# First channel block of a transformer layer modulated for two token tiles alone, with its value weights split in halves

## The chip, the cores and the metric

The kernel runs on one core of a Trainium2 chip. The metric is the device time of one execution in microseconds. One core has five engines that work side by side, each from a queue of its own: TensorE (matrix products and transposes; PE in the profile, with its weight loads as PEld), VectorE (DVE), ScalarE (ACT), GpSimd (POOL) and SyncE (SP), which here issues the loads and stores. TensorE writes to PSUM, and VectorE or ScalarE copy from there to SBUF.

## The reference, cut to what matters

One layer of a hybrid block over 512 latent tokens (`x`) and 256 context tokens (`ctx`) with 1024 channels. The part that the change touches is the start:

```python
mod = jax.nn.silu(c) @ ada_w[l] + ada_b[l]
sh1, sc1, g1, sh2, sc2, g2 = split(mod, 6)          # the same with c_ctx for the context tokens
hx = rmsnorm(x, norm1_g[l]) * (1 + sc1) + sh1        # (512, 1024)
hc = rmsnorm(ctx, norm1_g[l]) * (1 + csc1) + csh1    # (256, 1024)
v   = (hx @ w_in[l])[:, values]                      # (512, 512), one of the products with w_in
v_c = (hc @ w_in[l])[:, values]                      # (256, 512)
...
```

Then follow the other products with `w_in` (a Fourier mixer, a gated convolution, neighbourhood attention that reads the context keys too, three gates), the merged branches with an output product, a second modulated norm, a squared-ReLU MLP of width 4096 and a final norm.

## The kernel before

**Precision.** Every product is done in three matmuls (`mm3`, lines 82 to 84). Each operand is held as two parts, a high part (a cast, ScalarE, line 59 or 200) and a low part (the operand minus the high part, VectorE, line 60 or 201). Line 82 multiplies high by high, 83 high by low, 84 low by high.

**The head of the kernel.** Tokens are on partitions in tiles of 128: four latent tiles `xts` and two context tiles `cts`. `token_norm` takes a tile: ScalarE squares and sums it (148), VectorE and GpSimd make the reciprocal root (103, 104), VectorE scales the tile (150), TensorE turns it in two groups of four transposes (154), and VectorE copies the first group and ScalarE the second (155) to `xnT` (latent) or `cnT` (context), where channels are on partitions. Channels come in eight blocks of 128, numbered `m`.

Scale and shift of a block come in two steps. The row step `mod_rows(m)` is 16 matmuls with the weights `adaA[m]` (163) and a copy to SBUF `rsb` (166). The column step `mod_cols(m)` is four small matmuls that turn the rows (172) and two small VectorE instructions for `a1` and `b1` (173, 174). Then `modulate(m)` does block `m` for all tokens: one VectorE instruction (177), the cast (59) and the low part (60) to `hx` or `hc`. `values(m, wv, ts)` adds block `m` to the value products of the token tiles `ts`, three matmuls for each tile into one of six PSUM accumulators `vacc`.

The value weights come in loads of 1024 columns that serve two blocks: the first 512 columns block `m`, the others block `m + 1`; `halves` makes both parts of all 1024 (200, 201).

**Order before the loop.** Norms of latent tiles 0 and 1, row step of block 0, norms of tiles 2 and 3, column step of block 0, modulation of block 0 for all 512 tokens, parts of the first value weights. The loop over `m` then does in turn the loads for later blocks, the row step of block `m + 1`, the products of tiles 0 and 1, the column step and the modulation of block `m + 1`, and the products of tiles 2 and 3. At `m == 1` the context tiles are normed and join.

**What sets the order.** The program states dependences; a planner decides, when the kernel is built, in which order each engine gets its instructions. It goes by the order of the program among those that it reckons ready, so an instruction can stand in an engine's queue well ahead of its place in the text, as the cast of the value weights does (it is ahead of tile copies that are written before it). At run time each engine takes its queue strictly in that order. `tc.keep_in_program_order(ins)` ties an instruction to a place behind the one that was traced just before it on the same engine; it orders the queue and adds no wait for another engine.

**Loads.** SyncE issues them in its own order. The weights `adaA` go through four buffers, two for each block, so that the loads for block `m + 2` wait for the row step of block `m`; the value weights go through two buffers. The latent tiles and `adaA[0]` come first, then `wV[0]`, `adaA[1]`, `adaA[2]` and the context tiles.

Of the kernel before, what the change touches and what calls it, by code (L numbers as in the profile page):

```python
# [11 lines left out]
F32R = mybir.dt.float32r  # L12
AF = mybir.ActivationFunctionType
ALU = mybir.AluOpType
PSUM = bass.MemoryType.PSUM

P = 128
D = 1024
SEQ = 512
# [7 lines left out]
KD = D // P  # L27
# [3 lines left out]
HT = SEQ // 2  # L31
RAW = 4 * HALF
# [5 lines left out]
def dit_block(ctx: ExitStack, tc: tile.TileContext, a: dict):  # L38
    nc = tc.nc
    PE, V, S, G = nc.tensor, nc.vector, nc.scalar, nc.gpsimd  # L40

    def pool(stack, name, bufs, side=None, space=None):
        kw = {"reuse_waits": "tile"}
        if side:
            kw["side"] = side
        if space:
            kw["space"] = space
        return stack.enter_context(tc.tile_pool(name=name, bufs=bufs, **kw))
# [3 lines left out]
    wsp = pool(ctx, "wsp", 3)  # L52
    sgp = pool(ctx, "sgp", 3)

    def f(ap):
        return ap.bitcast(F32)

    def split(hi, lo, src):
        S.copy(hi, src)  # L59
        V.tensor_tensor(lo, src, f(hi), op=ALU.subtract)  # L60

    def weights(src, n=D):

        raw = wraw.tile([P, RAW], F32, tag="raw", name="raw")
        nc.sync.dma_start(raw[:, :n], src)
        w = weight_tile()
        split(w[:, 0, :n], w[:, 1, :n], raw[:, :n])
        return w
# [11 lines left out]
    def mm3(out, st, mv, start, stop, **kw):  # L80

        PE.matmul(out, st[0], mv[0], start=start, stop=False, **kw)  # L82
        PE.matmul(out, st[0], mv[1], start=False, stop=False, **kw)  # L83
        PE.matmul(out, st[1], mv[0], start=False, stop=stop, **kw)  # L84
# [17 lines left out]
    def rstd_of(ss, n):  # L102
        V.tensor_scalar(ss, ss, 1.0 / D, EPS, op0=ALU.mult, op1=ALU.add)  # L103
        G.tensor_tensor(ss, ss, mhalf[:, 0:n], op=ALU.pow)  # L104
# [7 lines left out]
    a1 = const.tile([P, KD, 2], F32, name="a1")  # L112
    b1 = const.tile([P, KD, 2], F32, name="b1")
# [3 lines left out]
    hx = hxp.tile([P, 2, KD, SEQ], F32R, name="hx")  # L117
# [19 lines left out]
    xnT = ph1.tile([P, KD, SEQ], F32, name="xnT")  # L137
    cnT = ph1.tile([P, KD, CTX], F32, name="cnT")

    def load(src, t):  # L140
        xt = ph1.tile([P, D], F32, tag="xt", name="xt", bufs=4)
        nc.sync.dma_start(xt, src[t * P:(t + 1) * P, :])
        return xt

    def token_norm(xt, t, dst):
        ss = ph1.tile([P, 1], F32, tag="ss", name="ss", bufs=3)
        junk = ph1.tile([P, D], mybir.dt.bfloat16, tag="junk", name="junk")
        S.activation(junk, xt, AF.Square, accum_out=ss)
        rstd_of(ss, 1)
        V.tensor_scalar(xt, xt, ss, None, op0=ALU.mult)  # L150
        for g in range(2):
            tp = ps1.tile([P, 4, P], F32, tag="acc", name="tp", bufs=6)
            for i in range(4):
                PE.transpose(tp[:, i, :], xt[:, (4 * g + i) * P:(4 * g + i + 1) * P], ident)
            (S.copy if g else V.tensor_copy)(dst[:, 4 * g:4 * g + 4, t * P:(t + 1) * P], tp)

    def mod_rows(m, w):


        rows = ps1.tile([P, 256], F32, tag="rows", name="rows")  # L160
        for k in range(KD):
            j = k % 4
            PE.matmul(rows[32 * j:32 * j + 32], sig32[:, k, :], w[k // 4][:, j * 256:(j + 1) * 256],
                      start=k < 4, stop=k >= 4)
        rsb = ph1.tile([P, 256], F32, tag="rsb", name="rsb", bufs=2)
        S.copy(rsb, rows)
        return rsb

    def mod_cols(m, rsb):
        cp = ps1.tile([P, 2, 2], F32, tag="cols", name="cp")  # L170
        for i in range(2):
            PE.matmul(cp[:, i, :], rsb[:, i * P:(i + 1) * P], comb, start=True, stop=True)
        V.tensor_scalar(a1[:, m, :], cp[:, 0, :], bsc1[:, m:m + 1], n1g[:, m:m + 1], op0=ALU.add, op1=ALU.mult)
        V.tensor_scalar(b1[:, m, :], cp[:, 1, :], bsh[:, m:m + 1], None, op0=ALU.add)

    def modulate(m, src, dst, j):
        V.tensor_scalar(src[:, m], src[:, m], a1[:, m, j:j + 1], b1[:, m, j:j + 1], op0=ALU.mult, op1=ALU.add)
        split(dst[:, 0, m], dst[:, 1, m], src[:, m])

    vacc = {}  # L180

    def values(m, w, ts):
        mv = [w[:, h, (m % 2) * 512:(m % 2 + 1) * 512] for h in range(2)]
        for t in ts:
            if m == 0:
                vacc[t] = ps1.tile([P, 512], F32, tag="acc", name=f"vacc{t}", bufs=6)
            if t < 4:
                st = [hx[:, h, m, t * P:(t + 1) * P] for h in range(2)]
            else:
                st = [hc[:, h, m, (t - 4) * P:(t - 3) * P] for h in range(2)]  # L190
            mm3(vacc[t], st, mv, m == 0, m == KD - 1)

    def fetch(src, p=rawx):
        raw = p.tile([P, RAW], F32, tag="raw", name="raw")
        nc.sync.dma_start(raw[:, :D], src)
        return raw[:, :D]

    def halves(raw):
        w = wsp.tile([P, 2, RAW], F32R, tag="w", name="w")
        S.copy(w[:, 0, :D], raw)  # L200
        V.tensor_tensor(w[:, 1, :D], raw, f(w[:, 0, :D]), op=ALU.subtract)
        return w

    def ada_fetch(m):
        return [fetch(a["adaA"][m, i]) for i in range(2)]

    xts = [load(a["x"], t) for t in range(2)]
    ada = ada_fetch(0)
    xts += [load(a["x"], t) for t in range(2, NT)]
    wn = fetch(a["wV"][0], wraw)  # L210
    w = ada
    ada = ada_fetch(1)
    token_norm(xts[0], 0, xnT)
    token_norm(xts[1], 1, xnT)
    rsb = mod_rows(0, w)
    token_norm(xts[2], 2, xnT)
    token_norm(xts[3], 3, xnT)
    mod_cols(0, rsb)
    modulate(0, xnT, hx, 0)
    wv = halves(wn)  # L220
    for m in range(KD):
        if m < KD - 1:
            w = ada
        if m % 2 == 1 and m < KD - 1:
            wn = fetch(a["wV"][(m + 1) // 2], wraw)
        if m < KD - 2:
            ada = ada_fetch(m + 2)
        if m == 0:
            cts = [load(a["ctx"], t) for t in range(NCT)]
        if m < KD - 1:  # L230
            rsb = mod_rows(m + 1, w)
        if m % 2 == 0 and m:
            wv = halves(wn)
        values(m, wv, range(2))
        if m < KD - 1:
            mod_cols(m + 1, rsb)
            modulate(m + 1, xnT, hx, 0)
        values(m, wv, range(2, 4))
        if m == 1:
            for t in range(NCT):  # L240
                token_norm(cts[t], t, cnT)
            modulate(0, cnT, hc, 1)
            modulate(1, cnT, hc, 1)
            values(0, wv, (4, 5))
        if m:
            values(m, wv, (4, 5))
            if m < KD - 1:
                modulate(m + 1, cnT, hc, 1)
    for t in range(6):
        src = vacc[t].rearrange("p (h d) -> p h d", d=HD)  # L250
        split(Vst[:, t, :, 0, :], Vst[:, t, :, 1, :], src)
# [63 lines left out]
    for g in range(2):  # L315
        w = weights(a["wU"][g])
# [19 lines left out]
    for c in range(2):  # L336
        pf = ps1.tile([P, 512], F32, tag="acc", bufs=6, name="pf")
        for half in range(2):
            for z in range(2):
                m = (0, 2 if half == 0 else 1)[z]  # L340
# [183 lines left out]
    for c in range(KD):  # L524
# [12 lines left out]
        w = weights(a["wM"][c])  # L537
# [67 lines left out]
    for kk in range(4):  # L605
        w = weights(a["wO"][0, kk])
# [9 lines left out]
    for kk in range(4):  # L616
        raw = wraw.tile([P, RAW], F32, tag="raw", name="raw")[:, :D]
        nc.sync.dma_start(raw, a["wO"][1, kk])
        w = wop.tile([P, 2, D], F32R, tag="wo", name="wo")
# [23 lines left out]
    def turned(t, xn):  # L643
        out = []
        for g in range(2):
            tp = psZ.tile([P, 4, P], F32, tag="d", name="tp2")
            for i in range(4):
                PE.transpose(tp[:, i, :], xn[:, (4 * g + i) * P:(4 * g + i + 1) * P], ident)
            out.append(tp)
        return out  # L650
# [282 lines left out]
    for ii in range(4):  # L933
        raw = wraw.tile([P, RAW], F32, tag="raw", name="raw")[:, :D]
        nc.sync.dma_start(raw, a["w2"][3, 1, ii])
        w = Sp.tile([P, 2, D], F32R, tag="S", name="wl", bufs=4)
        split(w[:, 0], w[:, 1], raw)
        ws.append(w)
    for t in range(NT):
        ss = sss[t]  # L940
# [110 lines left out]
```

## Time and profile before

| what | value |
|---|---|
| median of 3 runs | 802.93 us (802.64 to 803.0) |
| the profiled execution | 803.09 us, its span 801.3 us |
| TensorE matmuls, busy | 782.6 us (98%), 4484 instructions |
| VectorE, busy | 525.4 us (66%), 792 instructions |
| ScalarE, busy | 346.7 us (43%), 587 instructions |
| GpSimd, busy | 110.7 us (14%), 127 instructions |
| chain that ended last | TensorE 93%, VectorE 2%, ScalarE 2% |

Times in the views count from the start of the span. A row of the timeline has the start, the duration, the engine, the line of the kernel, the operation, the output and the inputs; in square brackets stands how long the engine was idle before and what ended that. Merged instructions carry their number (x8). A low share of an engine's busy time says nothing about a stretch in which another engine waits for it.

### The profile page before, as it was taken

How to read it: one execution, taken by the hardware profiler on the slowest of the kernel's cores; microseconds unless marked ns; L12 is line 12 of the kernel's file. 1: busy time of each engine (PE TensorE's matmuls, PEld its weight loads, DVE VectorE, ACT ScalarE, POOL GpSimd, SP SyncE). 2: the span in 40 equal slices, each digit the busy share in tenths (PEclk: the TensorE clock that was granted, in tenths of full speed). 3: DMA queues.
4: the chain of work that ended last, by engine and by line, in shares of the span. 5: the costliest groups of instructions: out<-in, count | busy, mean ns of one | idle time of the engine just before them, and what ended most of it. 6: DMA issues, size and time to landing. Idle time of an engine off the chain costs nothing.

```text
span 801.3 us, 11393 instructions
## 1 busy us (share of the span) xinstructions
PE 782.6 (98%) x4484; PEld 673.7 (84%) x4484; DVE 525.4 (66%) x792; ACT 346.7 (43%) x587; POOL 110.7 (14%) x127
## 2 busy tenths in 40 slices
PE   4999999999999999999999999999999999999996
PEld 3679988888888888888888999989888989998885
DVE  4655455997977898444358988656556666475973
ACT  5435334564782322323245475344543444334232
POOL 1000002221201000000000014222222222032000
PEclk9999999999999999999999999999999999999998
DMA  8654232332309897322443132223233333321312
GB/s 330 250 193 109 80 116 69 99 95 80 83 29 321 299 313 254 124 95 89 157 157 133 53 133 79 95 90 113 98 106 106 106 106 106 106 80 54 125 60 105
DMA packets 33654, 104.07 MB, mean 130 GB/s; under 512 B 8128, under 2 KB 8256, under 8 KB 33600
## 3 DMA queue, kind: packets, MB, share of 16 engines
q1 hardware_dynamic: 32832, 100.97, 36.9%
q0 software_dynamic: 768, 2.38, 1.5%
q8 instruction: 35, 0.57, 0.3%
q14 instruction: 19, 0.16, 0.1%
HBM read 98.87 MB, written 2.10 MB: 126 GB/s over the span
## 4 chain that ended last, share of the span: by engine, by line
PE 93%; DVE 2%; ACT 2%; issue 1%; DMA 1%; SPq 0%; POOL 0%; POOLq 0%; ACTq 0%
PE pd L82 7%; PE pd L83 7%; PE pd L84 7%; PE pg L84 6%; PE pg L83 6%; PE pg L82 5%; PE pA L84 3%; PE pA L82 3%; PE pA L83 3%; PE pu L83 2%; PE pu L82 2%; PE pu L84 2%; PE pbr L83 2%; PE pbr L84 2%; PE pbr L82 2%; PE vacc L82 2%
## 5 line engine op out<-in xcount | busy, mean ns | idle before, releaser
L60 DVE TENSOR_TENSOR w<-raw,w 128x1024 fp32r<-128x1024 f32 x87 | 108.1, 1243 | 54.3 <-ACT w L59 53.3
L59 ACT CAST w<-raw 128x1024 fp32r<-128x1024 f32 x87 | 91.2, 1048 | 83.0 <-PE pbr L84 27.4
L60 DVE TENSOR_TENSOR w<-rr,w 128x512 fp32r<-128x512 f32 (+1 forms) x65 | 66.6, 1044 | 72.0 <-ACT w L59 70.7
L83 PE MATMUL pd<-w,aT 128*128 128x512 f32 x224 | 87.8, 392 | 0.0
L84 PE MATMUL pd<-w,aT 128*128 128x512 f32 x224 | 87.6, 391 | 0.0
L82 PE MATMUL pd<-w,aT 128*128 128x512 f32 x224 | 85.8, 394 | 0.0
L59 ACT CAST w<-rr 128x512 fp32r<-128x512 f32 (+1 forms) x65 | 45.0, 707 | 78.1 <-POOL rr L780 34.7
L84 PE MATMUL pg<-hx,w 128*128 128x512 f32 x192 | 76.5, 398 | 0.0
L83 PE MATMUL pg<-hx,w 128*128 128x512 f32 x192 | 76.2, 397 | 0.0
L82 PE MATMUL pg<-hx,w 128*128 128x512 f32 x192 | 74.9, 390 | 0.0
L84 PEld LDWEIGHTS pd<-w,aT 128*128 128x128 f32 x224 | 42.0, 187 | 9.4
L83 PEld LDWEIGHTS pd<-w,aT 128*128 128x128 f32 x224 | 42.1, 188 | 9.0 <-DVE w L60 0.8
L82 PEld LDWEIGHTS pd<-w,aT 128*128 128x128 f32 x224 | 41.8, 188 | 8.2 <-ACT w L59 0.4
L82 PEld LDWEIGHTS pg<-hx,w 128*128 128x128 f32 x192 | 36.8, 192 | 8.0
L83 PEld LDWEIGHTS pg<-hx,w 128*128 128x128 f32 x192 | 36.1, 188 | 8.0
L517 DVE SCALAR_TENSOR_TENSOR acc<-ada,sig,acc 128x1024 f32<-128x1024 f32 x28 | 35.9, 1283 | 10.3 <-DMA ada<-in_adaB 10.0
L776 POOL TENSOR_TENSOR rr<-rr 128x512 f32<-128x512 f32 x13 | 17.3, 1333 | 183.4 <-DVE w L60 183.4
L84 PEld LDWEIGHTS pg<-hx,w 128*128 128x128 f32 x192 | 36.1, 188 | 7.2
L104 POOL TENSOR_TENSOR ss<-ss,mhalf 128x1 f32<-128x1 f32 x10 | 6.6, 660 | 224.5 <-DVE ss L103 224.5
L534 ACT ACTIVATE sg<-pg 128x512 f32<-128x512 f32 x21 | 12.5, 597 | 58.0 <-PE pg L84 57.9
L544 DVE TENSOR_TENSOR sg<-pbr,sg 128x512 f32<-128x512 f32 x24 | 16.5, 686 | 20.6 <-PE pbr L84 20.6
L84 PE MATMUL pA<-Sq,w 128*128 128x256 f32 x104 | 29.3, 282 | 0.0
(338 smaller groups left out, 2151.5 us busy)
## 6 DMA issues: line engine op xcount, KB each, us to landing
raw<-in_w SPq DMA_DIRECT2D x38, 512.0 KB, 3.5
ada<-in_adaB SPq DMA_DIRECT2D x32, 512.0 KB, 5.1
rr<-in_w SPq DMA_DIRECT2D x26, 512.0 KB, 4.0
raw<-in_wG SPq DMA_DIRECT2D x24, 512.0 KB, 3.4
raw<-in_adaA SPq DMA_DIRECT2D x16, 512.0 KB, 6.3
raw<-in_wM SPq DMA_DIRECT2D x8, 512.0 KB, 3.9
raw<-in_wO SPq DMA_DIRECT2D x8, 512.0 KB, 3.3
raw<-in_wC SPq DMA_DIRECT2D x6, 512.0 KB, 3.3
```

The source lines that it names most:

```text
L59: S.copy(hi, src)
L60: V.tensor_tensor(lo, src, f(hi), op=ALU.subtract)
L82: PE.matmul(out, st[0], mv[0], start=start, stop=False, **kw)
L83: PE.matmul(out, st[0], mv[1], start=False, stop=False, **kw)
L84: PE.matmul(out, st[1], mv[0], start=False, stop=stop, **kw)
L104: G.tensor_tensor(ss, ss, mhalf[:, 0:n], op=ALU.pow)
L517: V.scalar_tensor_tensor(acc[:, q, :], raw, sigv[:, k, 0:1], acc[:, q, :], op0=ALU.mult, op1=ALU.add)
L534: S.activation(sg, pg, AF.Sigmoid)
L544: V.tensor_tensor(pgs[b], pb, pgs[b], op=ALU.mult)
L776: G.tensor_tensor(ra[:, lo], ra[:, lo], rb[:, lo], op=ALU.add)
```

## The change

Latent tile 2 is normed and scaled, but not turned, before the row step of block 0. The parts of the first value weights are made in halves: the first 512 columns early, the others behind the modulation of the second 256 tokens. Block 0 is modulated in two halves of 256 tokens, the first (tiles 0 and 1) before tile 2 is turned. The products of tiles 0 and 1 with block 0 and the row step of block 1 leave the loop and stand between the turning of tiles 2 and 3. `token_norm` is taken apart into `squares`, `scaled` and `turned`; the square and the scaling of tile 3 and the copies of tiles 2 and 3 are pinned with `in_order`, each behind the instruction that is traced before it on its engine. The context tiles still go through `token_norm` as a whole, unpinned.

```diff
--- before.py
+++ after.py
@@ -59,6 +59,10 @@
         S.copy(hi, src)
         V.tensor_tensor(lo, src, f(hi), op=ALU.subtract)
 
+
+
+    in_order = tc.keep_in_program_order
+
     def weights(src, n=D):
 
         raw = wraw.tile([P, RAW], F32, tag="raw", name="raw")
@@ -142,17 +146,27 @@
         nc.sync.dma_start(xt, src[t * P:(t + 1) * P, :])
         return xt
 
-    def token_norm(xt, t, dst):
+    def squares(xt):
         ss = ph1.tile([P, 1], F32, tag="ss", name="ss", bufs=3)
         junk = ph1.tile([P, D], mybir.dt.bfloat16, tag="junk", name="junk")
-        S.activation(junk, xt, AF.Square, accum_out=ss)
+        return ss, S.activation(junk, xt, AF.Square, accum_out=ss)
+
+    def scaled(xt, ss):
         rstd_of(ss, 1)
-        V.tensor_scalar(xt, xt, ss, None, op0=ALU.mult)
+        return V.tensor_scalar(xt, xt, ss, None, op0=ALU.mult)
+
+    def token_norm(xt, t, dst):
+        scaled(xt, squares(xt)[0])
+        turned(xt, t, dst)
+
+    def turned(xt, t, dst):
         for g in range(2):
             tp = ps1.tile([P, 4, P], F32, tag="acc", name="tp", bufs=6)
             for i in range(4):
                 PE.transpose(tp[:, i, :], xt[:, (4 * g + i) * P:(4 * g + i + 1) * P], ident)
-            (S.copy if g else V.tensor_copy)(dst[:, 4 * g:4 * g + 4, t * P:(t + 1) * P], tp)
+            copied = (S.copy if g else V.tensor_copy)(dst[:, 4 * g:4 * g + 4, t * P:(t + 1) * P], tp)
+            if dst is xnT and t >= 2:
+                in_order(copied)
 
     def mod_rows(m, w):
 
@@ -173,9 +187,9 @@
         V.tensor_scalar(a1[:, m, :], cp[:, 0, :], bsc1[:, m:m + 1], n1g[:, m:m + 1], op0=ALU.add, op1=ALU.mult)
         V.tensor_scalar(b1[:, m, :], cp[:, 1, :], bsh[:, m:m + 1], None, op0=ALU.add)
 
-    def modulate(m, src, dst, j):
-        V.tensor_scalar(src[:, m], src[:, m], a1[:, m, j:j + 1], b1[:, m, j:j + 1], op0=ALU.mult, op1=ALU.add)
-        split(dst[:, 0, m], dst[:, 1, m], src[:, m])
+    def modulate(m, src, dst, j, t=slice(None)):
+        V.tensor_scalar(src[:, m, t], src[:, m, t], a1[:, m, j:j + 1], b1[:, m, j:j + 1], op0=ALU.mult, op1=ALU.add)
+        split(dst[:, 0, m, t], dst[:, 1, m, t], src[:, m, t])
 
     vacc = {}
 
@@ -212,14 +226,26 @@
     ada = ada_fetch(1)
     token_norm(xts[0], 0, xnT)
     token_norm(xts[1], 1, xnT)
+    scaled(xts[2], squares(xts[2])[0])
+
     rsb = mod_rows(0, w)
-    token_norm(xts[2], 2, xnT)
-    token_norm(xts[3], 3, xnT)
+    wv = wsp.tile([P, 2, RAW], F32R, tag="w", name="w")
+    S.copy(wv[:, 0, :512], wn[:, :512])
+    ss3, sq = squares(xts[3])
+    in_order(sq)
     mod_cols(0, rsb)
-    modulate(0, xnT, hx, 0)
-    wv = halves(wn)
+    V.tensor_scalar(xnT[:, 0, :HT], xnT[:, 0, :HT], a1[:, 0, 0:1], b1[:, 0, 0:1], op0=ALU.mult, op1=ALU.add)
+    V.tensor_tensor(wv[:, 1, :512], wn[:, :512], f(wv[:, 0, :512]), op=ALU.subtract)
+    split(hx[:, 0, 0, :HT], hx[:, 1, 0, :HT], xnT[:, 0, :HT])
+    turned(xts[2], 2, xnT)
+    in_order(scaled(xts[3], ss3))
+    rsb = mod_rows(1, ada)
+    values(0, wv, range(2))
+    turned(xts[3], 3, xnT)
+    modulate(0, xnT, hx, 0, slice(HT, SEQ))
+    split(wv[:, 0, 512:D], wv[:, 1, 512:D], wn[:, 512:])
     for m in range(KD):
-        if m < KD - 1:
+        if m:
             w = ada
         if m % 2 == 1 and m < KD - 1:
             wn = fetch(a["wV"][(m + 1) // 2], wraw)
@@ -227,11 +253,12 @@
             ada = ada_fetch(m + 2)
         if m == 0:
             cts = [load(a["ctx"], t) for t in range(NCT)]
-        if m < KD - 1:
+        elif m < KD - 1:
             rsb = mod_rows(m + 1, w)
         if m % 2 == 0 and m:
             wv = halves(wn)
-        values(m, wv, range(2))
+        if m:
+            values(m, wv, range(2))
         if m < KD - 1:
             mod_cols(m + 1, rsb)
             modulate(m + 1, xnT, hx, 0)
```

## Rows read from the trace of the kernel before

**Rows 1.** The page's busy times: us, share of the span, number of instructions.

```profile
PE 782.6 (98%) x4484; PEld 673.7 (84%) x4484; DVE 525.4 (66%) x792; ACT 346.7 (43%) x587; POOL 110.7 (14%) x127
```

**Rows 2.** Stretches: us; busy (instructions) PE, PEld, DVE, ACT, POOL; granted clock; DMA share; GB/s.

```profile
12.60:19.50 6.90, 5.20 (x55) 3.55 (x54) 5.82 (x13) 5.10 (x10) 1.10 (x2) 1.00 1.00 382
...
27.00:29.00 2.00, 1.70 (x12) 0.96 (x9) 1.68 (x3) 1.61 (x3) 0.28 (x1) 1.00 0.88 336
29.00:785.00 756.00, 755.17 (x4296) 652.28 (x4295) 505.19 (x747) 327.00 (x550) 104.41 (x109) 1.00 0.37 122
```

**Rows 3.** Timeline, TensorE's steps from 14 to 23 us.

```profile
14.08 1.09 PE L154 MATMUL tp<-ident,xt 128*128 128x128 f32 x8 [0.39 <-DVE xt L150]
...
15.01 0.51 PE L172 MATMUL cp<-cols,rsb 128*128 128x2 f32 x4
...
16.75 1.07 PE L163 MATMUL rows<-raw,sig 128*32 128x256 f32 x16
...
19.54 0.50 PE L82 MATMUL vacc<-w,hx 128*128 128x512 f32 x1 [0.61 <-ACT hx L59]
...
22.51 1.07 PE L163 MATMUL rows<-raw,sig 128*32 128x256 f32 x16
```

**Rows 4.** The same timeline, instructions around them from 12 to 21 us.

```profile
12.62 1.06 PE L163 MATMUL rows<-raw,sig 128*32 128x256 f32 x14
...
12.79 1.06 ACT L148 ACTIVATE junk<-xt 128x1024 bf16<-128x1024 f32 x1
...
14.31 0.38 ACT L166 COPY rsb<-rows 128x256 f32<-128x256 f32 x1
14.58 1.06 ACT L200 CAST w<-raw 128x1024 fp32r<-128x1024 f32 x1
14.86 0.75 DVE L150 TENSOR_SCALAR xt<-xt,ss 128x1024 f32<-128x1024 f32 x1 [0.73 <-POOL ss L104]
...
16.13 0.27 DVE L173 TENSOR_SCALAR a<-cp,bsc,cols 128x2 f32<-128x2 f32 x1
16.42 0.69 DVE L155 COPY xnT<-tp 128x512 f32<-128x512 f32 x1
...
17.03 0.21 DVE L174 TENSOR_SCALAR b<-cp,cols 128x2 f32<-128x2 f32 x1
17.16 1.21 DVE L201 TENSOR_TENSOR w<-raw,w 128x1024 fp32r<-128x1024 f32 x1
...
18.86 0.62 ACT L59 CAST hx<-xnT 128x512 fp32r<-128x512 f32 x1 [0.60 <-DVE xnT L177]
...
20.70 0.62 ACT L59 CAST hx<-xnT 128x512 fp32r<-128x512 f32 x1 [1.22 <-DVE xnT L177]
```

**Rows 5.** Groups by line and shape, first 50 us: count, busy us, mean ns.

```profile
L60 DVE TENSOR_TENSOR hx<-xnT,hx 128x512 fp32r<-128x512 f32 x6 | 4.1, 688 | 0.8 <-ACT hx L59 0.7
...
L59 ACT CAST hx<-xnT 128x512 fp32r<-128x512 f32 x6 | 3.7, 620 | 8.1 <-DVE xnT L177 8.1
...
L177 DVE TENSOR_SCALAR xnT<-xnT,a,b 128x512 f32<-128x512 f32 x6 | 3.3, 545 | 0.1
...
L177 DVE TENSOR_SCALAR cnT<-cnT,a,b 128x256 f32<-128x256 f32 x6 | 2.3, 408 | 0.0
...
L59 ACT CAST hc<-cnT 128x256 fp32r<-128x256 f32 x6 | 2.2, 406 | 0.0
L60 DVE TENSOR_TENSOR hc<-cnT,hc 128x256 fp32r<-128x256 f32 x5 | 1.9, 420 | 0.0
```

**Rows 6.** Timeline of SyncE: when the loads were issued.

```profile
4.29 0.57 SPq L195 DMA_DIRECT2D raw<-in_wV  x1
...
14.16 0.90 SPq L142 DMA_DIRECT2D xt<-in_ctx  x2
```

**Rows 7.** Loads issued near 4.3 us: count, KB, us to landing.

```profile
raw<-in_wV SPq DMA_DIRECT2D x1, 512.0 KB, 9.5
```

**Rows 8.** Loads issued near 14.2 us.

```profile
xt<-in_ctx SPq DMA_DIRECT2D x1, 512.0 KB, 6.0
```

## The prediction

> **What bounds the kernel now.** I read the page's busy shares first. TensorE's matmul row is busy for 782.6 us of a span of 801.3 us [rows 1]; only 18.7 us of the whole span can be won without taking matmuls away. The table by stretches then says where those are. From 29 us to 785 us the engine is busy for 755.17 of 756.00 us [rows 2], so nothing that is moved about there can gain. The change lies in the first 30 us, and of these the stretch 12.6 to 19.5 us holds 5.20 us of TensorE work in 6.90 us, 1.70 us idle; 27 to 29 us holds another 0.30 us [rows 2]. The reader should see in this the ceiling of the whole idea: the same matmuls are run before and after, TensorE is full from 19.5 us on, so the end of the kernel moves by as much as the idle TensorE time of the head shrinks or grows, and by no more than about 2.0 us downwards. The granted clock is 1.00 in each of these stretches [rows 2], so it plays no part.
>
> The timeline of TensorE shows what the idle time waits for: the transposes of token tile 2 (14.08), the column step of modulation block 0 (15.01), then the transposes of tile 3, the row step of block 1 (16.75) and its column step, and at 19.54 the first value product [rows 3]. The value products of block 0 fill 19.54 to 22.51, where the row step of block 2 follows [rows 3]. The timeline of the other engines says why 19.54: block 0 is modulated for all 512 tokens in one instruction, behind the four tiles' copies and behind the low half of 1024 weight columns, which holds VectorE from 17.16 for 1.21 us; ScalarE's cast of the modulated block at 18.86 releases the product [rows 4].
>
> **The change part by part.** *Tiles 0 and 1 alone.* The row step of block 0 ends at 12.62 + 1.06 = 13.68 [rows 4]. Its copy to SBUF ran at 14.31, since the square of tile 3 (12.79, 1.06 us) and a tile copy stood ahead of it on ScalarE [rows 4]. With that square pinned behind the weight cast, the copy can run at 13.75 and end (0.38 us [rows 4]) near 14.15. The cast of the first 512 weight columns costs what a cast of 128x512 costs, 0.62 us [rows 5], and its data landed 9.5 us after an issue at 4.29, so at 13.8 [rows 6, 7]: it ends near 14.75. The column step stays where it is (15.01 to 15.52), because the transposes of tile 2 are ready at 14.08 [rows 3] and the copy it needs comes a little later. The two small VectorE instructions behind it (0.27 and 0.21 us [rows 4]) end at 16.0. The modulation of 256 tokens costs 0.41 us in place of 0.545, its cast 0.41 in place of 0.62 [rows 5]. So the first six products can start at 16.0 + 0.41 + 0.41, about 16.85, and not at 19.54: 2.7 us earlier.
>
> *What the other half pays.* The square of tile 3 begins at 14.75 and not at 12.79, 1.96 us late. From the start of that square to the start of the scaling is 14.86 - 12.79 = 2.07 us [rows 4], so by this path the scaling could run at 16.8. But it is pinned behind VectorE's copy of tile 2, and that behind the low half of the modulated block. On VectorE after 16.4 stand: the low half of 512 weight columns (0.69, by the 128x512 row), the low half of 256 tokens (0.42) [rows 5], the copy of tile 2 (0.69 [rows 4]): 18.2. The pin decides, not the square. Then the scaling of tile 3 (0.75 [rows 4]): 18.95; four of eight transposes (half of 1.09 [rows 3]): 19.5; the copy 0.69: 20.2, against 16.42 + 0.69 = 17.11 before [rows 4]; modulation and cast of the second 256 tokens, 0.82: about 21.05. The second six products start there, and last half of the 2.97 us between 19.54 and 22.51 [rows 3], so they end at 22.55. Where the first half wins 2.7 us, the second loses 1.5 us, and block 0's products end where they ended.
>
> *What TensorE does meanwhile.* From 16.85 to 21.05 it has the row step of block 1 (1.07), six products (1.49), the column step (0.51) and the transposes of tile 3 (1.09) [rows 3]: 4.16 us of work for 4.2 us. That gap is closed. What stays is 0.4 us before the transposes of tile 2 (13.68 to 14.08), and the time from 15.52 to the next piece of work. That is the row step of block 1, which began at 16.75 with no wait for its data shown [rows 3]. When those data were there isn't in these rows: between 15.52 (no idle time) and 16.75 (1.23 us idle); I take the middle, some 0.65 us, since the copies and casts begin before the end of the one ahead of them and the products can't come much under 16.6 either. Idle after: 0.4 + 0.65 and a little for the joints, 1.2 us, against 1.70. **Gain 0.5 us**; bounds 0.05 us (start at 16.75) and 1.3 us (no idle after 15.52).
>
> *The split instructions* themselves: casts of 256 tokens twice 0.406 - 0.620 = 0.19; modulation twice 0.408 - 0.545 = 0.27; low halves twice 0.420 - 0.688 = 0.15 [rows 5]; the weight cast twice 0.62 - 1.06 = 0.18; its low half twice 0.69 - 1.21 = 0.17 [rows 4, 5]. That is 0.37 us more for ScalarE and 0.59 us for VectorE. I cost them at nothing beyond the sums above, because the second weight half isn't read before block 1's products and TensorE has its 4.16 us of other work; without that cover the price is their sum, 0.96 us. The Trainium skill, page "VectorE: DVE Perf Modes", section "The TRN2 errata", speaks against such splitting: each instruction that reads SBUF pays a fixed latency, so it advises tiles of 512 elements or more, and here tiles of 512 become tiles of 256. The rows agree that halving doesn't halve the time (0.406 against 0.620). By that rule alone the edit costs time, by the rows above it is covered.
>
> *The queues.* The loads of block 2's modulation weights wait for the row step of block 0, which stays at 13.68; those of block 3 wait for the row step of block 1, which moves by at most 0.6 us either way. The context tiles are issued behind the first of these at 14.16 and land 6.0 us later, at 20.2 [rows 6, 8]. Nothing new is queued on SyncE, and GpSimd has only the four small power instructions. In ScalarE's queue the pinned square stands behind the weight cast, and the cast of the modulated half waits behind the square: free at 14.75 + 1.06 = 15.8 [rows 4] and the reading of its sum, needed at 16.4. That wait costs nothing as long as the weights land by 14.2.
>
> **The sum.** The profiled execution took 803.09 us with a span of 801.3; the median of the runs is 802.93, 0.16 us under it. 803.09 - 0.5 = 802.6 for such an execution, 802.4 on the scale of the median. Within 0.2% means within 1.6 us here, about what a measurement of this kernel can tell from none.
>
> **The rivals.** *Splitting lands on the path.* If the second half isn't covered, as when the transposes of tile 3 slip behind the row step, VectorE's and ScalarE's extra 0.96 us show in place of a gain of 0.5: 802.93 + 0.96 - 0.5 = 803.4. For it: the chain to 21.05 has no slack against TensorE's 4.2 us. Against it: half of the extra instructions serve block 1, at 22 us or later. The page named above would put the time here.
>
> *All idle time goes.* The planner also puts the row step of block 2 into what gaps are left, and the 0.30 us at 27 to 29 us [rows 2] goes: 1.70 + 0.30 = 2.0 us, 800.9. Against it: at 15.52 nothing is ready that doesn't wait for a load or for the modulation chain.
>
> *The context squares get ahead* (slower). The change pins squares and copies of the latent tiles but not those of the context tiles. ScalarE is now free near 20 us, waiting for tile 3, and the planner may put the context squares there. The first lands at 20.2 and holds ScalarE 1.06 us to 21.3; a second tile of 512 KB at the 382 GB/s of the loads [rows 2] lands some 1.4 us later, at 21.6, and would hold it to 22.7. The cast of the second 256 tokens then ends at 23.1 and not at 21.05: 2.05 us, with nothing gained 805.0. It decides over the forecast when both squares are ahead and the row step of block 2 isn't there to fill the gap; one square alone costs 0.65 us, which leaves the time within 0.2%. For it: nothing in the diff holds these squares back. Against it: in the kernel before, ScalarE sat idle for 1.22 us before the cast at 20.70 [rows 4], although the first context tile had landed at 20.2, and no square was put there.
>
> **How the numbers follow.** Forecast (gain 0.05 to 1.3 us) 0.48; splitting on the path (803.0 to 803.9) 0.24; all idle time gone (1.6 us or more) 0.15; context squares ahead (1.6 us or more lost) 0.13. The first two are the case within 0.2%, with 0.01 of the forecast's upper end given to faster: 0.16 faster, 0.71 same, 0.13 slower. The range runs from 801.1, which leaves out the better half of the third case, to 804.1, beyond which lies most of the fourth: some 0.2 left out. The likeliest case alone holds 801.6 to 802.9.
>
> **What would show it.** Right: the first products on TensorE near 16.9 (six of them), the row step of block 1 near 16.2, tile 3's scaling near 18.9, the second six products near 21 and their end near 22.5; TensorE's idle time in 12.6 to 19.5 us near 1.2 us; from 29 us on a busy share as before, only shifted. Wrong: a gap of over half a microsecond on TensorE between 17 and 23 us, with the cast of the second half late behind a context square or behind the second weight half; or block 0's products ending under 21.5. The forecast fails as a whole if the order of work after 30 us changes and idle time appears there, which the stretch from 29 us on would show.

## The result and the profile after

The changed kernel takes 809.45 us (median of 4 runs, 808.21 to 809.56) where the kernel before takes 802.96 us beside it (4 runs, 802.64 to 803.34): 0.8% slower, ratio 1.0081 (95% interval 1.0069 to 1.0093). The forecast was 802.4 with a range from 801.1 to 804.1. The profiled execution took 809.41 us, its span 807.6 us, 6.3 us more than the span of before.

The page's busy times of the kernel after answer to [rows 1]:

```profile
PE 786.6 (97%) x4484; PEld 675.4 (84%) x4484; DVE 525.7 (65%) x795; ACT 347.9 (43%) x589; POOL 110.7 (14%) x127
```

TensorE runs the same 4484 matmuls, yet it is busy 4.0 us longer and idle 2.3 us longer (807.6 - 786.6 against 801.3 - 782.6). Both matter. Of the 4.0 us, 1.6 are slow matmuls behind 130 us (below), 0.8 lie between the end of block 0's row step and the first product behind the value products (51.03 us busy from 14.40 to 67.25, before 50.27 from 13.68 to 65.99), and 1.4 ahead of that end, in the first row step and the 16 transposes, whose pace differs from execution to execution (last section). The stretches of the kernel after, with the columns of [rows 2]:

```profile
12.60:19.50 6.90, 5.95 (x45) 3.20 (x48) 3.98 (x11) 3.93 (x8) 0.55 (x1) 1.00 0.87 307
19.50:27.00 7.50, 6.94 (x53) 4.69 (x47) 4.61 (x11) 4.46 (x9) 0.55 (x1) 1.00 1.01 389
27.00:29.00 2.00, 2.00 (x14) 1.68 (x12) 1.23 (x5) 1.11 (x2) 0.55 (x1) 1.00 0.96 330
...
125.00:130.00 5.00, 1.79 (x15) 1.61 (x14) 2.87 (x5) 2.27 (x4) 0.00 (x0) 1.00 0.00 0
130.00:135.00 5.00, 5.00 (x16) 3.92 (x16) 0.00 (x0) 0.00 (x0) 0.00 (x0) 0.66 0.32 105
...
135.00:785.00 650.00, 649.16 (x3644) 562.76 (x3642) 450.14 (x653) 285.93 (x476) 99.55 (x98) 1.00 0.37 122
```

The reader should see three things. From 135 us on nothing has changed: 649.16 us busy of 650, and 649.17 in the same stretch of before. In the head the idle time of 12.6 to 19.5 us fell from 1.70 to 0.95 us, but 0.56 us came up in 19.5 to 27. And at 125 us, a hundred microseconds behind the last line of the diff, TensorE stands idle for 3.21 us, and in the 5 us behind that it does only 16 matmuls where before did 30, at a granted clock of 0.66. The list of TensorE's waits (us in total, times, longest) names the place, in the line of `pu`; before has no such line:

```profile
...
PE pu L86 <- DVE Kst L333: 3.2, 1, 3.2
PE vacc L86 <- ACT hx L59: 0.6, 1, 0.6
...
```

**The wait at 126 us.** `pu` is the accumulator of the first convolution projection, the first tile of the attention part. `Kst` is the copy of the last attention keys out of the accumulator `pc`, cast by line 332 (ScalarE) and given its low part by line 333 (VectorE). The timelines of TensorE, ScalarE and VectorE of the kernel after around it:

```profile
126.35 0.28 PE L88 MATMUL pc<-hc,w 128*128 128x256 f32 x1
...
126.94 1.04 ACT L59 CAST w<-raw 128x1024 fp32r<-128x1024 f32 x1
128.00 0.37 ACT L332 CAST Kst<-pc 64x256 fp32r<-64x256 f32 x1
...
128.01 1.23 DVE L60 TENSOR_TENSOR w<-raw,w 128x1024 fp32r<-128x1024 f32 x1 [0.53 <-ACT w L59]
129.27 0.43 DVE L333 TENSOR_TENSOR Kst<-pc,Kst 64x256 fp32r<-64x256 f32 x1
...
129.84 0.56 PE L86 MATMUL pu<-hx,w 128*128 128x512 f32 x1 [3.21 <-DVE Kst L333]
130.20 0.63 PE L87 MATMUL pu<-hx,w 128*128 128x512 f32 x1
130.62 0.63 PE L88 MATMUL pu<-hx,w 128*128 128x512 f32 x1
...
133.18 0.54 PE L88 MATMUL pu<-hx,w 128*128 128x512 f32 x1
133.56 0.40 PE L86 MATMUL pu<-hx,w 128*128 128x512 f32 x1
```

And the kernel before, where the same instructions stand in the same order on each engine (lines 82 to 84, 305 and 306 are the same code):

```profile
125.08 0.29 PE L84 MATMUL pc<-hc,w 128*128 128x256 f32 x1
...
125.21 0.39 PE L82 MATMUL pu<-hx,w 128*128 128x512 f32 x1
...
125.41 0.37 ACT L305 CAST Kst<-pc 64x256 fp32r<-64x256 f32 x1 [0.95 <-PE pc L84]
125.44 0.39 PE L83 MATMUL pu<-hx,w 128*128 128x512 f32 x1
...
126.75 0.37 ACT L305 CAST Kst<-pc 64x256 fp32r<-64x256 f32 x1
126.76 1.23 DVE L60 TENSOR_TENSOR w<-raw,w 128x1024 fp32r<-128x1024 f32 x1 [0.53 <-ACT w L59]
```

In before `pu` begins 0.13 us behind the start of the last matmul of `pc`, long before the copies of `pc` are done. After, it waits for the last of them, and that one stands behind the cast and the low part of 1024 weight columns (1.04 and 1.23 us), which nobody had to hurry before. The first nine matmuls of `pu` then take 3.72 us (129.84 to 133.56), where one follows the next after 0.23 us in before: 2.08 us for nine, so 1.64 us more. Counted by the starts, `pu` comes 3.49 us behind the last matmul of `pc` instead of 0.13, so 3.36 us are lost there and 1.64 behind it. The last matmul of `pc` itself is 1.27 us late (126.35 against 125.08), which comes from the head. Together that is 6.27 of the 6.3 us.

What differs is where the two tiles lie in PSUM, which the profile doesn't show and the built programs do. The accumulators of the first part rotate through six banks; each tile takes the bank that came free, so the order in which early tiles are opened and closed decides every later one. Before, the first four `vacc` lie in banks 4, 1, 3, 2; the change opens two of them ahead of tile 3's transposes, and they lie in 0, 5, 2, 3. Down the line the last `pc` moves from bank 4 to bank 0. `pu` comes from another pool, `psP`, opened first in the attention part, and lies in bank 0 in both kernels. A tile that takes over a bank must not be written before the last reader of the tile ahead of it is done, so the program lets `pu` start only behind the copies of `pc` when both lie in one bank.

**The head.** TensorE in the kernel after, to be read against [rows 3]:

```profile
14.89 0.61 PE L186 MATMUL cp<-cols,rsb 128*128 128x2 f32 x4 [0.49 <-ACT rsb L180]
15.36 1.07 PE L166 MATMUL tp<-ident,xt 128*128 128x128 f32 x8
16.36 0.64 PE L177 MATMUL rows<-raw,sig 128*32 128x256 f32 x8
16.93 0.50 PE L86 MATMUL vacc<-w,hx 128*128 128x512 f32 x1
...
18.60 0.33 PE L166 MATMUL tp<-ident,xt 128*128 128x128 f32 x1 [0.47 <-DVE xt L156]
18.93 0.49 PE L88 MATMUL vacc<-w,hx 128*128 128x512 f32 x1
19.35 0.64 PE L177 MATMUL rows<-raw,sig 128*32 128x256 f32 x8
19.92 0.51 PE L88 MATMUL vacc<-w,hx 128*128 128x512 f32 x1
...
22.66 0.50 PE L86 MATMUL vacc<-w,hx 128*128 128x512 f32 x1 [0.56 <-ACT hx L59]
...
24.82 0.50 PE L86 MATMUL vacc<-w,hx 128*128 128x512 f32 x1
```

The first product starts at 16.93. But only four of the six come there, the row steps are cut in two (0.64 us for each half, 1.07 for a whole one in [rows 3]), the second six products start at 22.66, and block 1's products at 24.82; in before these follow the row step that starts at 22.51 [rows 3], at 23.51. The context transposes come at 28.17 instead of 26.84, so in these two executions the head hands on a delay of 1.3 us. Not all of it can be put down to the change: block 0's row step ended at 14.40 (12.72 + 1.68) against 13.68, 0.7 us later, ahead of the reordered work on TensorE. VectorE shows what holds up the products:

```profile
16.91 0.15 DVE L107 TENSOR_SCALAR ss<-ss 128x1 f32<-128x1 f32 x1
17.79 0.75 DVE L156 TENSOR_SCALAR xt<-xt,ss 128x1024 f32<-128x1024 f32 x1 [0.73 <-POOL ss L108]
18.45 0.42 DVE L60 TENSOR_TENSOR hx<-xnT,hx 128x256 fp32r<-128x256 f32 x1
18.79 0.68 DVE L167 COPY xnT<-tp 128x512 f32<-128x512 f32 x1
```

The scaling of tile 3 (L156) stands ahead of the low half of tiles 0 and 1 (L60) and of the copy of tile 2 (L167). VectorE waits 0.73 us for GpSimd's root while work that is ready stands behind. The low half ends at 18.87, and the two products that read it (L88) come at 18.93 and 19.92.

### The profile page after: what moved, and what is told of

Same layout as the page of the kernel before. It is cut to its first block, busy times and chain, and to the rows that moved or that the text cites. A ratio compares the mean times of both kernels' runs of the same rounds, so it can differ in the third digit from the quotient of the medians.

```text
span 807.6 us, 11397 instructions
## 1 busy us (share of the span) xinstructions
PE 786.6 (97%) x4484; PEld 675.4 (84%) x4484; DVE 525.7 (65%) x795; ACT 347.9 (43%) x589; POOL 110.7 (14%) x127
## 4 chain that ended last, share of the span: by engine, by line
PE 93%; ACT 2%; DVE 2%; issue 1%; DMA 1%; SPq 0%; POOL 0%; POOLq 0%; ACTq 0%
PE pd L86 7%; PE pd L87 7%; PE pd L88 7%; PE pg L88 5%; PE pg L87 5%; PE pg L86 5%; PE pA L88 3%; PE pA L87 3%; PE pA L86 3%; PE pu L87 2%; PE pu L86 2%; PE pu L88 2%; PE pbr L87 2%; PE pbr L88 2%; PE pbr L86 2%; PE pC L88 2%
## 5 line engine op out<-in xcount | busy, mean ns | idle before, releaser
L60 DVE TENSOR_TENSOR w<-raw,w 128x1024 fp32r<-128x1024 f32 (+2 forms) x88 | 108.9, 1237 | 53.7 <-ACT w L59 53.7
L59 ACT CAST w<-raw 128x1024 fp32r<-128x1024 f32 (+2 forms) x88 | 91.8, 1044 | 84.1 <-PE pbr L88 19.3
L60 DVE TENSOR_TENSOR w<-rr,w 128x512 fp32r<-128x512 f32 (+1 forms) x65 | 66.6, 1044 | 71.6 <-ACT w L59 70.3
L88 PE MATMUL pd<-w,aT 128*128 128x512 f32 x224 | 87.6, 391 | 0.0
L88 PE MATMUL pg<-hx,w 128*128 128x512 f32 x192 | 76.5, 398 | 0.0
L88 PEld LDWEIGHTS pd<-w,aT 128*128 128x128 f32 x224 | 42.0, 187 | 9.3
L88 PEld LDWEIGHTS pg<-hx,w 128*128 128x128 f32 x192 | 36.1, 188 | 7.2
L88 PE MATMUL pA<-A,w 128*128 128x256 f32 x104 | 29.3, 282 | 0.0
```

## The experiments

Two theories stood after this. *Banks*: about 5 us come from `pu` falling on the bank of the last `pc`, and the head costs about 1.3. *Order*: the reordered head delays the weights or the keys, and the wait at 126 us is a late consequence of it, not of the bank. The control for the first is to move the bank and nothing else.

**e1, after with the pools in another order.** One line is moved, which gives `pu` bank 3:

```diff
-    psP = pool(gt, "psP", 2, space=PSUM)
     psT = pool(gt, "psT", 3, space=PSUM)
+    psP = pool(gt, "psP", 2, space=PSUM)
     psO = pool(gt, "psO", 1, space=PSUM)
```

> The changed kernel with one edit far behind the change: the PSUM pool of the attention's transposes is opened ahead of the pool of its projections, so that the first convolution projection gets bank 3 (read out long before) and not bank 0, which in the changed kernel holds the context keys of the last head pair until they are copied. Bank theory: the wait of 3.2 us near 126 us and the granted clock of 0.66 behind it both go, about 4.9 us in all, and 1.3 us from the head stay: 804.2 to 804.7 us. Rival, the keys' copies themselves or the changed head make that projection late: the wait stays near 3 us and the time near 809.4 us.

Measured 803.99 us (11 runs, 802.92 to 804.53) against 802.78 (27 runs), ratio 1.0014 (1.0006 to 1.0023). The wait is gone from TensorE's list, and the two stretches are full again at full clock:

```profile
125.00:130.00 5.00, 5.00 (x28) 4.30 (x27) 2.77 (x4) 2.02 (x4) 0.00 (x0) 1.00 0.03 9
130.00:135.00 5.00, 5.00 (x30) 4.18 (x29) 2.57 (x6) 2.95 (x6) 1.01 (x2) 1.00 0.27 96
```

The head's order is the one of after, to the instruction. Of 6.49 us lost, 1.21 stay: the bank cost 5.3 us and the head 1.2. The median is a little under the forecast of 804.2 to 804.7.

**e2, before with the collision.** The opposite: the kernel before with the pools opened as `psT`, `psO`, `psP`, `psS`, which gives `pu` bank 4, the one that its last `pc` has.

> The kernel before, with nothing of the change, only its attention pools opened in another order (transposes, output, projections, scores), so that the first convolution projection gets bank 4, which there holds the context keys of the last head pair. Bank theory: a wait of about 3.2 us on TensorE behind the last key projections and a lower granted clock after it, 807.5 to 808.2 us. Rival, the wait comes from the changed head: no such wait and 802.9 us.

Measured 806.78 us (5 runs, 805.86 to 807.99), ratio 1.0047 (1.0034 to 1.0059). The same wait, to the hundredth, in a kernel whose head is untouched:

```profile
127.53 0.47 PE L82 MATMUL pu<-hx,w 128*128 128x512 f32 x1 [3.21 <-DVE Kst L306]
...
129.01 0.63 PE L82 MATMUL pu<-hx,w 128*128 128x512 f32 x1
```

The collision alone makes the kernel before lose the time, so the order theory falls. The median is below the forecast of 807.5 to 808.2. In the profiled execution the slow matmuls are there (the first 14 took 4.88 us, 127.53 to 132.41, 1.65 us over 14 times 0.23; the last eight of them are the slow ones). The two shortest runs, 805.96 and 805.86, lie 3.1 us over before, about the wait alone, and have a mean clock of 0.999 over the whole execution, the other three 0.995 to 0.997. That fits a loss of clock which doesn't come in every run; those two runs have no trace, so it isn't shown.

**e3, control.** Before with the pool order of e1, where no collision is made or mended.

> Control: the kernel before with the same pool order as the first of these runs (transposes ahead of projections); its first convolution projection gets bank 3, read out early. Both theories: 802.9 us, within 0.3 us. If the pool order has a price of its own, it shows here.

Measured 802.67 us (11 runs), ratio 0.9997 (0.9988 to 1.0006). The order of the pools costs nothing by itself.

With the same pools, e1 and e3 also show what the changed head costs. The stretch from the end of block 0's row step to the first product behind the value products (`pus`, of the Fourier mixer) takes 52.86 us in e1 and 51.56 in e3 (first e1, then e3, with the columns of [rows 2]):

```profile
14.00:66.86 52.86, 51.04 (x321) 36.65 (x321) 32.96 (x71) 26.09 (x49) 1.65 (x3) 1.00 0.62 220
13.40:64.96 51.56, 50.15 (x323) 36.90 (x321) 32.43 (x67) 24.77 (x45) 1.48 (x3) 1.00 0.63 228
```

That is 1.30 us more, and the medians are 1.32 apart. Of it 0.89 us are the same matmuls being busy for longer, and only 0.41 are idle time (1.82 against 1.41). Against the trace of before (52.31 us, 50.27 busy) the stretch of e1 is 0.55 us longer, again by busy time (0.77) and not by idle time (0.22 less).

**e4, a pin that does what the text says.** `in_order` ties an instruction behind the one that was traced just before it on its engine. For `in_order(scaled(...))` that is the small VectorE instruction of `rstd_of` (L107), which `scaled` itself issues, and not the copy of tile 2. On e1, this traces the root earlier, so that the scaling is tied behind the copies of tile 2:

```diff
+    rstd_of(ss3, 1)
     turned(xts[2], 2, xnT)
-    in_order(scaled(xts[3], ss3))
+    in_order(V.tensor_scalar(xts[3], xts[3], ss3, None, op0=ALU.mult))
```

> The first of these runs, and the scaling of token tile 3 pinned where the description puts it: its reciprocal root is traced ahead of the turning of tile 2, so that the scaling itself is tied behind the copy of tile 2 and no longer stands ahead of the low half of the first two tiles on VectorE. Theory that the head loses time to VectorE's order (VectorE sits 0.73 us behind the scaling while the low half, and with it two products on TensorE, wait from 16.85 to 18.45 us): 0.3 to 0.8 us less than the first run, 803.5 to 804.2 us. Rival, the head loses because TensorE's own queue is cut up (row steps in halves, column step ahead of the transposes): within 0.2 us of the first run.

Measured 803.32 us (11 runs), ratio 1.0003 (0.9994 to 1.0012), 0.67 us under e1 on the same chip, within the 0.3 to 0.8 that were expected. VectorE no longer waits for the root; copy, low half and scaling (L242) follow each other:

```profile
17.03 0.15 DVE L107 TENSOR_SCALAR ss<-ss 128x1 f32<-128x1 f32 x1
17.09 0.68 DVE L167 COPY xnT<-tp 128x512 f32<-128x512 f32 x1
17.69 0.41 DVE L60 TENSOR_TENSOR hx<-xnT,hx 128x256 fp32r<-128x256 f32 x1
18.02 0.75 DVE L242 TENSOR_SCALAR xt<-xt,ss 128x1024 f32<-128x1024 f32 x1
```

The second six products start 6.99 us behind the column step of block 0 (22.00 and 15.01), in e1 7.78 us (22.26 and 14.48). About half of the head's loss is this pin. The other half, in this trace, is busy time: the stretch that took 51.56 us in e3 takes 52.05, of which TensorE is busy for 50.69 and idle for 1.36.

**e5, no pins at all.** e1 with `def in_order(ins): return ins`.

> The changed kernel with the repaired banks (as the first run) and every pin taken off: squares, copies and the scaling of tile 3 go where the planner puts them. If the pins carry the loss in the head (tile 3 held back by them), the time falls to 802.8 us or less. If the head loses because TensorE's queue is cut up (row steps in halves between other work), which the planner does without the pins too, it stays within 0.4 us of the first run's 804.0 us.

Measured 803.04 us (11 runs, 802.66 to 804.91) against 802.62 (33 runs), ratio 1.0010 (1.0001 to 1.0019). The pins of the change gain nothing: without them the head is no slower than with them (e1, 1.0014). The expectation named 802.8 or less, or within 0.4 of 804.0; the median lies between. Three of the eleven runs took 804.2 to 804.9 us, at a mean clock of 0.996 against 0.998 and 0.999 in the others; they have no trace, so that stays open. TensorE waits 1.1 us for the cast of `hx` and 0.7 us for a copy of the context tile.

**e6, TensorE's queue whole.** e4, and also the transposes of tile 2 ahead of column step 0, and the row steps of blocks 1 and 2 each kept whole behind the products, by a tie on each of their matmuls.

> Repaired banks; on TensorE the transposes of tile 2 are put ahead of the column step of block 0, and the row steps of blocks 1 and 2 behind the products traced before them, each in one piece; the scaling of tile 3 is truly tied behind the copy of tile 2. Theory of the cut queue: two cuts of a row step cost 0.24 us each (0.64 us for half a step, 1.07 for a whole one), and up to 0.5 us of idle time ahead of the column step goes, so 0.5 to 1.0 us less than the first run: 803.0 to 803.5 us. Rival, the halved modulation with its five extra instructions is what costs: no less than 803.8 us.

Measured 803.04 us (11 runs), ratio 1.0006 (0.9997 to 1.0015). The row steps of blocks 1 and 2 are whole, and TensorE waits for the casts of the two halves instead:

```profile
16.92 0.50 PE L86 MATMUL vacc<-w,hx 128*128 128x512 f32 x1 [1.63 <-ACT hx L59]
...
22.09 0.50 PE L86 MATMUL vacc<-w,hx 128*128 128x512 f32 x1 [1.13 <-ACT hx L59]
```

The median falls in the range that was expected, but e4, which has the same tie of the scaling, is there already (1.0003): the whole row steps add no gain. In the stretch from the end of block 0's row step TensorE is busy for 49.54 us instead of 50.69 (e4), and idle for 2.76 instead of 1.36. Cutting the steps cost about as much as it filled.

**e7, the cheap part of the idea in the kernel before.** No splitting. The low half of the first weights (1.21 us, [rows 4]) is tied behind the modulation of block 0, which it kept waiting (pool order of e3):

```diff
-    modulate(0, xnT, hx, 0)
-    wv = halves(wn)
+    V.tensor_scalar(xnT[:, 0], xnT[:, 0], a1[:, 0, 0:1], b1[:, 0, 0:1], op0=ALU.mult, op1=ALU.add)
+    wv = wsp.tile([P, 2, RAW], F32R, tag="w", name="w")
+    S.copy(wv[:, 0, :D], wn)
+    tc.keep_in_program_order(V.tensor_tensor(wv[:, 1, :D], wn, f(wv[:, 0, :D]), op=ALU.subtract))
+    split(hx[:, 0, 0], hx[:, 1, 0], xnT[:, 0])
```

> The kernel before with one edit in the head (and the pool order that was shown to cost nothing): the low half of the first value weights is tied behind the modulation of block 0, which in the kernel before it delays from 17.2 to 18.3 us. Nothing is halved, nothing else moved. If the start of block 0's products decides, as the prediction reasoned, they start up to 1.1 us earlier, where only the 0.6 us of idle time at 18.9 and part of the 0.5 us at 17.8 can be won: 802.0 to 802.4 us. If the head is bound by what TensorE has to do in any case, 802.8 us.

Measured 802.81 us (11 runs), ratio 1.0003 (0.9994 to 1.0012): no change, as the second of the two expectations said. Yet block 0's products start at 18.18 instead of 19.54, and block 1's at 22.64 instead of 23.51 (the column step of block 0 lies at 14.98 and 15.01; in e3 it lies at 14.27 and the products start at 18.50, so the gain is 1.0 to 1.4 us). The gain is given back at the context tiles, as TensorE and ScalarE of e7 show:

```profile
26.91 1.09 PE L154 MATMUL tp<-ident,xt 128*128 128x128 f32 x8 [0.77 <-DVE ss L103]
...
22.83 0.37 ACT L166 COPY rsb<-rows 128x256 f32<-128x256 f32 x1 [1.41 <-PE rows L163]
23.10 1.06 ACT L148 ACTIVATE junk<-xt 128x1024 bf16<-128x1024 f32 x1
```

The same two in before:

```profile
26.84 1.03 PE L154 MATMUL tp<-ident,xt 128*128 128x128 f32 x8
...
21.23 1.05 ACT L148 ACTIVATE junk<-xt 128x1024 bf16<-128x1024 f32 x1
```

The planner puts the copy of row step 2 ahead of the first context square, which so starts at 23.10; in before it started at 21.23. The transposes behind it come at 26.91, in before at 26.84.

**e8, weight halves alone.** Before (pool order of e3) with the first weights made in two halves of 512 columns, nothing else.

> The kernel before with one part of the change alone (and the same pool order): the first value weights made in two halves of 512 columns, block 0 modulated for all tokens at once as before, nothing pinned. The low half ahead of the modulation is 0.69 us and not 1.21, so the products of block 0 start 0.5 us earlier: 802.2 to 802.6 us. If the extra instructions cost more than they give, 802.8 us or more.

Measured 802.90 us (11 runs), ratio 1.0003 (0.9995 to 1.0012). A gain was expected and none came; the 0.28 us over before are inside the interval of no change. The first products did start earlier, as expected (3.77 us behind the column step of block 0, in before 4.53, in e3 4.23), but TensorE waits 0.77 us for the first context tile, as in e7. The halved modulation was not tested alone.

**e9, e7 with the context square held in front.** The square of the first context tile is traced ahead of row step 2, and the copy of that row step is tied behind it.

> The run with the weights behind the modulation, and one more tie: ScalarE's copy of block 2's row step goes behind the square of the first context tile, which in that run waited for it until 23.1 us and so left TensorE idle for 0.77 us before the transposes of that tile. If the context tile's chain took back what the head had won, the wait of 0.77 us goes and the time is 801.9 to 802.3 us, 0.3 to 0.8 us under the kernel before. If the tile's load or something else sets that moment, the time stays within 0.2 us of the kernel before.

Measured 803.75 us (11 runs) against 802.47 (15 runs), ratio 1.0014 (1.0005 to 1.0023), where 801.9 to 802.3 was expected. A miss. The square starts at 21.23 again and the first context transposes come at 25.86 with no wait, but the next chain is late instead. TensorE and VectorE of e9:

```profile
29.19 1.06 PE L158 MATMUL tp<-ident,xt 128*128 128x128 f32 x8 [1.74 <-DVE xt L154]
...
25.70 0.55 DVE L183 TENSOR_SCALAR xnT<-xnT,a,b 128x512 f32<-128x512 f32 x1
26.50 0.69 DVE L159 COPY cnT<-tp 128x512 f32<-128x512 f32 x1 [0.25 <-PE tp L158]
27.11 0.15 DVE L103 TENSOR_SCALAR ss<-ss 128x1 f32<-128x1 f32 x1
```

The second context tile's sum was there at 24.15, but the small instruction that begins its root (27.11) stands in VectorE's queue behind the modulation of block 2 and the copy of the first context tile. TensorE waits 1.74 us for what comes of it. One tie moved the wait by one tile and made it larger.

## Why the prediction was wrong

**The step that failed.** "TensorE is full from 19.5 us on, so the end of the kernel moves by as much as the idle TensorE time of the head shrinks or grows", and with it that from 29 us to 785 us "nothing that is moved about there can gain". A full stretch can't gain, but it can lose. It was full because each tile happened to lie in a bank that had come free, and the change shuffled the banks without touching an instruction there. No term of the sum and no rival had this: 5.3 of the 6.5 us (e1), and made again in the kernel before by the bank alone (e2). The text did say that idle time behind 30 us would sink the forecast; it is what happened, without the changed order that it had in mind.

The same step fails in the head too, with the bank mended. There the end moved by more than the idle time did: from e3 to e1 the stretch grew by 1.30 us and its idle time by 0.41. "The same matmuls" are not the same busy time when they are cut and reordered. A row step in two halves is shown at 0.64 us twice instead of 1.07, the first product behind other work at 0.50 instead of 0.40. The sum put this at nothing.

**The head, point by point.** The cast of 256 tokens in 0.41 us was right, and the chain from the column step to the first product nearly so (2.04 us, where 1.84 were reckoned). That this product came "about 16.85" (16.93) was luck: block 0's row step ended 0.72 us later than reckoned (14.40), and the column step did not stay behind the transposes of tile 2 but ran ahead of them, 0.49 us behind the end of the row step. Behind that end the first product comes after 2.53 us (2.52 in e1), where 3.17 were reckoned. The row step of block 1 near 16.2 (16.36) was luck as well: the prediction put 0.65 us of waiting for data ahead of it, and what lies there are the transposes of tile 2 (15.36). "The pin decides, not the square" was wrong. I read the pin as a tie to the copy of tile 2; it ties the scaling only to the instruction that `scaled` issues just before it, and the planner put the scaling ahead of the copy and of the low half. The low half was due behind the cast at 16.84 and came at 18.45. Two of the "first six products" slipped behind it. "The second six products start there", at 21.05, became 22.66, and "they end at 22.55" became 24.25. "That gap is closed" was wrong too: TensorE waited 0.47 us at 18.60 and 0.56 at 22.66. By the medians of e1 the head lost 1.2 us where 0.5 were to be gained; with the tie as I had read it (e4) it loses 0.54 by the medians, an amount that the interval doesn't tell from none.

**The rivals.** *Splitting lands on the path* comes nearest in mechanism for the head: with the bank mended the kernel takes 803.99, and that rival said 803.0 to 803.9. But its cause, the extra time of the split instructions, isn't shown: halving the weight parts alone cost nothing (e8), halving the modulation was not tested alone. The order on VectorE was half of it (e4). Its sum also takes both the 0.96 us and the gain of 0.5, where its words put the one in place of the other, and adds up the busy time of two engines that work side by side. *All idle time goes* was wrong: 0.95 us is left in 12.6 to 19.5 us, and 0.56 more came up behind. *The context squares get ahead* did not happen: the first context square of after starts at 23.45, behind both casts of block 0's second half and block 1.

**The ceiling.** "By no more than about 2.0 us downwards" was too generous in kind as well. e7 starts block 0's products 1.0 to 1.4 us earlier for the price of one tie and the end doesn't move: the context tiles' chain through ScalarE, VectorE and GpSimd gives TensorE its next work at the same time as before. No version here beat the kernel before.

**What stays open.** Of the head's 1.2 us, 0.67 go with the tie of e4. The other half was not taken away by any run: e4, e5 and e6 stand 0.4 to 0.5 us over before, e4 by busy time, the others by other waits, and differences of this size are at the edge of what the medians tell. And e2 lost less than its wait and its slow matmuls add up to in the trace (4.0 against 4.9 us, by the medians).

## What to carry to other kernels

When a change opens or closes PSUM tiles in another order, look up in the built program in which bank each later tile lies, and above all the first tile of each later pool: a bank shared with the pool's predecessor turns that one's last reader into TensorE's wait, however far from the edit. A stretch that is full can't gain, but its being full is a fact to be checked again after the change, not a bound on the loss. Idle time alone isn't what a reordering costs either: work that is cut into pieces can be busy for longer. And a tie to "the instruction before" is to be read by the trace of the program, helper functions included, before its effect is costed.

## What the runs showed of the hardware

The wait of 3.21 us cost half as much again. Behind it TensorE's matmuls of 128x512 followed each other after 0.43 us, and after 0.23 us later on; the granted clock over these 5 us was 0.66, a mean of the full level (2.4 GHz) and the half (1.2 GHz). Ahead of the fall TensorE had been full for over 25 us at 1.00 and then idle for 3.21 us. In the profile of e2 the fall came only at 129.0, after six matmuls at full pace, behind the same wait. The Trainium skill, page "Perfetto Trace Analysis", section "Matmul Optimizations", asks that matmuls be run back to back since the engine scales its power; the trace agrees, with 1.64 us lost behind the gap. The same page, section "Optimizing Tensor Performance", says that independent groups of matmuls should rotate through different banks so that one group's evacuation lies under the next group's matmuls. The trace agrees: 3.21 us with one bank, nothing with two.

The start of TensorE varied between executions by more than the change was worth: the first row step began at 8.83 us in the profile of before and at 8.16 in that of after, and the 16 transposes behind it took 2.90 us in the one and 3.67 in the other, the rest of the row step 1.06 and 1.68, with the granted clock shown as 1.00 in both. Single profiles of a head like this one can't be compared to better than half a microsecond; the medians can.
